# A merge stage whose stationary operand is swapped: activations stay in TensorE, weights stream

## The chip, the cores and the metric

The kernel runs on one core of one Trainium2 chip. The metric is the device time of one launch, in microseconds (us). Three runs of the kernel before gave 2219.97, 2220.11 and 2220.32 us; the median is 2220.11 us.

## The reference, cut to what matters

One layer works on 256 tokens of width 2048: a half-step SwiGLU feed-forward network (FFN), a token mixer, and a second such FFN, each with RMSNorm before and after it. The mixer has three branches (forgetting attention of width 1024, differential attention of 512, memory cross-attention of 512). The part that is changed merges them:

```python
gates = jax.nn.sigmoid(h @ w_merge_gate[l] + b_merge_gate[l])      # [256, 3 * 2048]
g_fox, g_diff, g_mem = jnp.split(gates, 3, axis=-1)
merged = (g_fox * (y_fox @ w_branch_fox[l])
          + g_diff * (y_diff @ w_branch_diff[l])
          + g_mem * (y_mem @ w_branch_mem[l]))                     # [256, 2048]
x = x + rmsnorm(merged @ w_out[l], mix_post_g[l])
```

## The kernel before

Every weight is float32 in memory and is multiplied in three passes: it is split into `hi` (rounded to the float32r format that TensorE multiplies) and `lo = raw - hi`, the activations are held split in the same way, and hi·hi, hi·lo and lo·hi are summed in PSUM. `Stream` does the splitting for all weights in one fixed order. SP (SyncE's queue) loads 1 MB tiles into 3 `raw` buffers (L71); each tile makes two pieces; for a piece ACT (ScalarE) casts `hi` (L94) and DVE (VectorE) subtracts `lo` (L95) into one of 4 split buffers. `ahead()` queues splits of pieces up to 4 beyond the last one released, and `load()` queues the raw tile that follows. So on every engine the order is that of the code: a split stands in the queue behind whatever was written before it, and waits there for the split buffer that PE (TensorE) has to release.

A product takes one of two forms. `mm_a` (L214, L216) keeps 128x128 of the weight stationary and streams the activations: one matmul of 512 columns (both halves of the activation, 256 tokens each) with `hi`, one of 256 columns with `lo`. Its result has channels on partitions, so it can be the next product's operand. `mm_b` (L241 to L243) keeps 128 tokens of an activation stationary and streams 512 columns of the weight: three matmuls for each token half, 12 for a piece. Its result has tokens on partitions and must be turned before it can be the next operand. The FFNs do that in `ffn_up`: DVE transposes 32x32 blocks (L443), `regroup` (L449) moves them with 16 small DMAs on SP, and `split` casts and subtracts (L297, L298). These steps are put into the next product of the FFN, after its pieces 1 and 6.

The mixer's `qk` products, its gates and its branch products use `mm_a`; the order is 16 rounds over blocks of 128 channels (`m`), each with three gate products (16 k-tiles each) and 16 k-tiles of branch products. `lr_sum` (L419, L421) adds the two halves of a bank, `times_row` (L428) multiplies by the token scale, L963 applies the sigmoid with the bias as a column, and L966, L968 multiply and add. `split_to` (L297, L298) writes the merged block `mT`, which the output product `PostProj("out", ...)` then reads k-tile by k-tile. Attention steps (`Fillers`) are slipped in after half products until the first gates are done. `h2T`, `y_a` and `y_b` begin 8 elements behind a 256-byte line (`OFF`), the `v` weights 28 elements behind one (`OFF_V`). Small row vectors such as `g_row` (L375) are loaded by DMAs that ACT issues.

Of the kernel before, what the change touches and what calls it, by code (L numbers as in the profile page):

```python
# [26 lines left out]
LAM_INIT = 0.8 - 0.6 * math.exp(-0.3 * 0)  # L27
NEG = -1e30


LINE = 256
OFF = 8
OFF_V = 28

C_G1, C_GM, C_GMEM, C_G2, C_B, C_HG = 0, 16, 32, 48, 64, 112
N_COLS = 113


class Stream:
# [78 lines left out]
def tile_block(ctx, tc, x, mem, f1gu, f1d, wqk, wv, wmkv, wgate, wbr, wout, f2gu, f2d,  # L118
# [42 lines left out]
        st.add("v", wv[i])  # L161
    for i in range(20):
        st.add("qk", wqk[i])
    for m in range(KT):
        for b in range(3):
            st.add("gate", wgate[b * KT + m])
        st.add("br", wbr[m])
    for i in range(16):
        st.add("out", wout[i], extra={12: (1,), 13: (0, 1)}.get(i, ()))
    add_up(2, f2gu)  # L170
# [30 lines left out]

    fill = Fillers(3, 2)

    def rows_of(pool, n, off, **kw):

        t = pool.tile([P, n * 2 * S + OFF], F32R, align_bytes=LINE, **kw)
        return t[:, off:off + n * 2 * S].rearrange("p (k s n) -> p k s n", k=n, s=2)


    def mm_a(bank, w, kk, act, k, start, stop):  # L210
# [7 lines left out]
    def new_bank(name):  # L218
        return mmp.tile([P, 512], F32, tag="mm", name=name)

    def proj_a(name, act):
        bank = new_bank("mm_a")
        for half in range(2):
            st.ahead()
            w, = st.take(name)
            for kk in range(8):
                k = half * 8 + kk
                mm_a(bank, w, kk, act, k, k == 0, k == KT - 1)
            st.release()
            fill()  # L230
        return bank
# [62 lines left out]
    def split_to(hi, lo, src, scale=None):  # L294

        if scale is None:
            nc.scalar.copy(out=hi, in_=src)  # L297
            nc.vector.tensor_tensor(out=lo, in0=src, in1=hi.bitcast(F32), op=ALU.subtract)  # L298
        else:
            nc.scalar.activation(out=hi, in_=src, func=AF.Copy, scale=scale)  # L300
            nc.vector.scalar_tensor_tensor(out=lo, in0=src, scalar=scale, in1=hi.bitcast(F32),
                                           op0=ALU.mult, op1=ALU.subtract)
# [113 lines left out]
    def lr_sum(dst, bank, tmp_pool, scale=1.0):  # L416

        left = tmp_pool.tile([P, S], F32, tag="left", name="left", bufs=2)
        nc.scalar.activation(out=left, in_=bank[:, 0:S], func=AF.Copy, scale=scale)  # L419
        if scale == 1.0:  # L420
            nc.vector.tensor_tensor(out=dst, in0=bank[:, S:2 * S], in1=left, op=ALU.add)  # L421
        else:
            nc.vector.scalar_tensor_tensor(out=dst, in0=bank[:, S:2 * S], scalar=scale, in1=left,
                                           op0=ALU.mult, op1=ALU.add)

    def times_row(dst, row):
        if row is not None:
            nc.vector.tensor_tensor(out=dst, in0=dst, in1=row, op=ALU.mult)  # L428


    def ffn_up(idx, hT, rstd, setup, groups, inserts):

        state = {}

        def gated(t, bank):
            nc.scalar.activation(out=state["s"][:, t], in_=bank, func=AF.Silu, scale=rstd[t])

        def product(t, bank):

            sg = state["s"]  # L440
            nc.vector.scalar_tensor_tensor(out=sg[:, t], in0=bank, scalar=rstd[t], in1=sg[:, t],
                                           op0=ALU.mult, op1=ALU.mult)
            nc.vector.transpose(out=state["z"][:, t], in_=sg[:, t])  # L443

        def regroup():

            for a in range(4):
                for q in range(4):
                    nc.sync.dma_start(out=state["w"][32 * q:32 * q + 32, :, a],  # L449
                                      in_=state["z"][32 * a:32 * a + 32, :, P * q:P * (q + 1)])  # L450

        def split(n):
            src = state["w"].rearrange("p t a (k i) -> p k (t a) i", k=4)
            hi, lo = (state["gh"][:, 4 * n:4 * n + 4, i].rearrange("p k (g i) -> p k g i", i=32) for i in range(2))
            for k in range(4):
                split_to(hi[:, k], lo[:, k], src[:, k])

        def open_block():
            for name, shape in (("s", [P, 2, 512]), ("z", [P, 2, 512]), ("w", [P, 2, 4, P])):
                state[name] = state["tp"].tile(shape, F32, tag="f" + name, name="f" + name, bufs=1)  # L460

        late = {}
        for n in range(FB):
            if n == 0:
                bg, bu = proj_b2(f"gu{idx}", hT, groups, inserts)
                state["tp"], state["gh"] = setup()
                open_block()
                for t in range(2):
                    gated(t, bg[t])
            else:  # L470
                bg = proj_b(f"gate{idx}", hT, KT, 512, steps=late)
                open_block()
                for t in range(2):
                    gated(t, bg[t])
                bu = proj_b(f"up{idx}", hT, KT, 512)
            for t in range(2):
                product(t, bu[t])
            late = {1: regroup, 6: lambda n=n: split(n)}
        return state["gh"], late


# [2 lines left out]
    hpool = h1_stack.enter_context(tc.tile_pool(name="hT1", bufs=1, side="right", reuse_waits="tile"))  # L484
    gp1 = g1_stack.enter_context(tc.tile_pool(name="gh1", bufs=1, side="left", reuse_waits="tile"))
    tp1 = g1_stack.enter_context(tc.tile_pool(name="ft1", bufs=1, side="left", reuse_waits="tile"))
    hT1 = rows_of(hpool, KT, 0, name="hT1")
    gh1 = rows_of(gp1, FT, 0, name="gh1")
    zeros = hpool.tile([P, 512], BF16, name="zeros")
    nc.vector.memset(zeros, 0.0)  # L490

# [48 lines left out]
    yap = ya_stack.enter_context(tc.tile_pool(name="yap", bufs=1, side="right", reuse_waits="tile"))  # L540
    fg_stack = ExitStack()
    fgp = fg_stack.enter_context(tc.tile_pool(name="fg1", bufs=1, side="right", reuse_waits="tile"))
    mha = rows_of(yap, 8, 0, tag="y", name="mha")
    macc = [small.tile([P, 4], F32, name=f"macc{t}", bufs=1) for t in range(2)]
    order = [(c, t) for c in range(4) for t in range(2)]
    mem_c = {}
# [27 lines left out]
    h2_stack = ExitStack()  # L574
    h2p = h2_stack.enter_context(tc.tile_pool(name="h2p", bufs=1, side="left", reuse_waits="tile"))
    ybp = yb_stack.enter_context(tc.tile_pool(name="ybp", bufs=1, side="left", reuse_waits="tile"))
    h2T = rows_of(h2p, KT, OFF, tag="h", name="h2T")
    mhb = rows_of(ybp, 8, 0, tag="y", name="mhb")

    def x1_update(i):  # L580
        if i < 8:
# [166 lines left out]

        return [s1, s2]

    y_a = rows_of(yap, 8, OFF, tag="y", name="y_a")
    y_b = rows_of(ybp, 8, OFF, tag="y", name="y_b")

    def softmax_stats(s_aps, tag="e", bufs=6):

# [175 lines left out]
            fill.add(mem_unit(h // 2, head("mq", sc)), 2)  # L931


    mg_stack = ExitStack()
    mT = None
    for m in range(KT):
        zs = []
        for b in range(3):
            z = zp.tile([P, S], F32, tag="z", name="z", bufs=4)
            lr_sum(z, proj_a("gate", h2T), zp)  # L940
            times_row(z, hrow)
            zs.append(z)
        if m == 0:
            while fill.left():
                fill(drain=True)
            at_stack.close()
            mgp = mg_stack.enter_context(tc.tile_pool(name="mgp", bufs=1, side="left", reuse_waits="tile"))
            mT = rows_of(mgp, KT, 0, name="mT")
        bb = [new_bank("mm_br") for _ in range(3)]
        lims = [(0, 8), (8, 12), (12, 16)]  # L950
        for half in range(2):
            st.ahead()
            w, = st.take("br")
            for kk in range(8):
                k = half * 8 + kk
                i = 0 if k < 8 else (1 if k < 12 else 2)
                mm_a(bb[i], w, kk, (y_a, y_b)[half], kk, k == lims[i][0], k == lims[i][1] - 1)
            st.release()
        acc = None
        for b in range(3):  # L960
            g = zs[b]
            c = C_B + b * KT + m
            nc.scalar.activation(out=g, in_=g, func=AF.Sigmoid, bias=colt[:, c:c + 1])  # L963
            br = zp.tile([P, S], F32, tag="br", name="br")
            lr_sum(br, bb[b], zp)
            nc.vector.tensor_tensor(out=g, in0=br, in1=g, op=ALU.mult)  # L966
            if acc is not None:
                nc.vector.tensor_tensor(out=g, in0=acc, in1=g, op=ALU.add)  # L968
            acc = g
        split_to(mT[:, m, 0], mT[:, m, 1], acc)  # L970
    mix.close()
    ya_stack.close()


    h3T = rows_of(h2p, KT, 0, tag="h", name="h3T")
    fg_stack = ExitStack()
    fgp = fg_stack.enter_context(tc.tile_pool(name="fgm", bufs=1, side="right", reuse_waits="tile"))
    st.extra_pool = fg_stack.enter_context(tc.tile_pool(name="xsplit", bufs=st.extra_bufs, side="right", reuse_waits="tile"))
# [9 lines left out]
        for c in range(4):  # L988
            post2.update(0, c)

    post2.body()
    banks = post2.last(lag=7, first_done=first_half,
                       inserts={1: lambda: x2_in(0, 0)(), 2: lambda: x2_in(0, 1)(), 3: lambda: st.ahead(2),
                                5: lambda: st.ahead(2)})
# [4 lines left out]
    def setup2():  # L999
        fg_stack.close()  # L1000
        mg_stack.close()
        yb_stack.close()
        gp = g2_stack.enter_context(tc.tile_pool(name="gh2", bufs=1, side="right", reuse_waits="tile"))
        tp = g2_stack.enter_context(tc.tile_pool(name="ft2", bufs=1, side="right", reuse_waits="tile"))
        return tp, rows_of(gp, FT, 0, name="gh2")

    gh2, late2 = ffn_up(2, h3T, h3r, setup2, [[0, 1]] + [[i] for i in range(2, 8)],
                        {(1, 0): lambda: (x2_in(1, 0, 2)(), post2.update(1, 1)),
# [109 lines left out]
```

## Time and profile before

| | |
|---|---|
| median of 3 runs | 2220.11 us |
| profiled execution, its own time | 2220.04 us |
| its span | 2218.2 us (1.8 us lie around it) |
| PE matmul busy | 2208.0 us, 100% of the span |
| DVE, ACT busy | 1288.2 us (58%), 1037.0 us (47%) |
| TensorE clock granted | 0.999 of full speed (2.4 GHz) |
| DMA engines, mean busy share | about half of the span in every slice |

A busy PE means that matmuls were under way, and their records overlap; what a matmul costs is the distance from its start to the next one's start, and is read from places far apart and a count between them.

### The profile page before, as it was taken

The numbers are of one execution on the slowest core, as the hardware profiler recorded it, in microseconds if no ns is written. First come the engines' busy times: TensorE is split into PE (matmuls) and PEld (weight loads), VectorE is DVE, ScalarE is ACT, GpSimd is POOL, SyncE is SP. The second block draws the span as 40 slices with busy tenths as digits, with TensorE's granted clock in tenths as the row PEclk, the third lists the DMA queues.
The fourth block names the chain that finished last, engine by engine and source line by source line (L and its number), as shares of the span: only waits on it lengthen the run. The fifth ranks groups of instructions, "written<-read, shape, count | busy, mean of one in ns | idle before, by whom it ended". The sixth has DMA issues, their size and how long they took to land. (4 is left out here: it accounts for less than half of the span.)

```text
span 2218.2 us, 27157 instructions
## 1 busy us (share of the span) xinstructions
PE 2208.0 (100%) x10625; PEld 1869.7 (84%) x10625; DVE 1288.2 (58%) x1625; ACT 1037.0 (47%) x1484; POOL 13.5 (1%) x25
## 2 busy tenths in 40 slices
PE   9999999999999999999999999999999999999998
PEld 7888888888888899988888888888888888888887
DVE  5555555555444756766776767566555555554444
ACT  6444444445344644544555555446444444444442
POOL 0000000000000000000000000000000000000000
PEclk9999999999999999999999999999999999999999
DMA  7565556566555454544555555654655565565553
GB/s 265 189 220 202 200 190 234 199 217 219 193 201 202 160 194 152 183 161 143 190 177 203 177 203 177 212 199 161 236 200 203 197 219 207 187 225 199 201 202 133
DMA packets 91793, 434.51 MB, mean 196 GB/s; under 512 B 13072, under 2 KB 35984, under 8 KB 44304
## 3 DMA queue, kind: packets, MB, share of 16 engines
q1 hardware_dynamic: 87200, 425.84, 54.9%
q10 hardware_dynamic: 4464, 6.93, 1.0%
q8 instruction: 83, 1.36, 0.2%
q14 instruction: 46, 0.38, 0.1%
HBM read 419.09 MB, written 2.10 MB: 190 GB/s over the span
## 5 line engine op out<-in xcount | busy, mean ns | idle before, releaser
L95 DVE TENSOR_TENSOR lo<-raw,hi 128x1024 fp32r<-128x1024 f32 (+2 forms) x794 | 957.0, 1211 | 760.2 <-ACT hi L94 756.3
L94 ACT CAST hi<-raw 128x1024 fp32r<-128x1024 f32 (+2 forms) x794 | 819.2, 1037 | 871.6 <-PE mm_b L243 761.9
L214 PE MATMUL mm_a<-h2T,hi 128*128 128x512 f32 x1088 | 384.0, 394 | 0.0
L216 PE MATMUL mm_a<-h2T,lo 128*128 128x256 f32 x1088 | 306.5, 282 | 0.0
L241 PE MATMUL mm_b<-hi,hT 128*128 128x512 f32 x704 | 274.3, 390 | 0.2 <-ACT hi L94 0.2
L241 PE MATMUL mm_b<-hi,h3T 128*128 128x512 f32 x704 | 274.5, 390 | 0.0
L242 PE MATMUL mm_b<-lo,hT 128*128 128x512 f32 x704 | 274.0, 389 | 0.5 <-DVE lo L95 0.5
L241 PE MATMUL mm_b<-hi,gh 128*128 128x512 f32 x704 | 274.2, 390 | 0.0
L243 PE MATMUL mm_b<-hi,h3T 128*128 128x512 f32 x704 | 274.0, 389 | 0.0
L243 PE MATMUL mm_b<-hi,hT 128*128 128x512 f32 x704 | 273.9, 389 | 0.0
L242 PE MATMUL mm_b<-lo,h3T 128*128 128x512 f32 x704 | 273.9, 389 | 0.0
L243 PE MATMUL mm_b<-hi,gh 128*128 128x512 f32 x704 | 273.9, 389 | 0.0
L242 PE MATMUL mm_b<-lo,gh 128*128 128x512 f32 x704 | 273.8, 389 | 0.0
L214 PEld LDWEIGHTS mm_a<-h2T,hi 128*128 128x128 f32 x1088 | 204.3, 188 | 42.1
L216 PEld LDWEIGHTS mm_a<-h2T,lo 128*128 128x128 f32 x1088 | 205.7, 189 | 0.2
L241 PEld LDWEIGHTS mm_b<-hi,hT 128*128 128x128 f32 x704 | 132.1, 188 | 28.2 <-ACT hi L94 0.7
L242 PEld LDWEIGHTS mm_b<-lo,hT 128*128 128x128 f32 x704 | 132.1, 188 | 28.1 <-DVE lo L95 0.8
L243 PEld LDWEIGHTS mm_b<-hi,gh 128*128 128x128 f32 x704 | 132.2, 188 | 27.6
L242 PEld LDWEIGHTS mm_b<-lo,h3T 128*128 128x128 f32 x704 | 132.2, 188 | 27.4
L243 PEld LDWEIGHTS mm_b<-hi,h3T 128*128 128x128 f32 x704 | 132.2, 188 | 27.4
L243 PEld LDWEIGHTS mm_b<-hi,hT 128*128 128x128 f32 x704 | 132.1, 188 | 27.4
L242 PEld LDWEIGHTS mm_b<-lo,gh 128*128 128x128 f32 x704 | 132.2, 188 | 27.3
(210 smaller groups left out, 1963.4 us busy)
## 6 DMA issues: line engine op xcount, KB each, us to landing
raw<-in_f2gu SPq DMA_DIRECT2D x88, 1024.0 KB, 5.0
raw<-in_f1gu SPq DMA_DIRECT2D x86, 1024.0 KB, 5.0
raw<-in_wgate SPq DMA_DIRECT2D x48, 1024.0 KB, 4.9
raw<-in_f1d SPq DMA_DIRECT2D x44, 1024.0 KB, 4.8
raw<-in_f2d SPq DMA_DIRECT2D x44, 1024.0 KB, 4.8
raw<-in_wv SPq DMA_DIRECT2D x24, 856.0 KB, 4.5
raw<-in_wqk SPq DMA_DIRECT2D x20, 1024.0 KB, 4.8
raw<-in_wbr SPq DMA_DIRECT2D x16, 1024.0 KB, 4.8
```

Of the source, the lines that this page charges most:

```text
L94: self.nc.scalar.copy(out=hi[:, i], in_=src[:, i])
L95: self.nc.vector.tensor_tensor(out=lo[:, i], in0=src[:, i], in1=hi[:, i].bitcast(F32), op=ALU.subtract)
L214: nc.tensor.matmul(bank, lhsT=hi[:, i, c], rhs=act[:, k].rearrange("p s n -> p (s n)"), start=start, stop=False)
L216: nc.tensor.matmul(bank[:, 0:S], lhsT=lo[:, i, c], rhs=act[:, k, 0], start=False, stop=stop)
L241: nc.tensor.matmul(o, lhsT=xh, rhs=wh, start=start and kk == 0, stop=False)
L242: nc.tensor.matmul(o, lhsT=xh, rhs=wl, start=False, stop=False)
L243: nc.tensor.matmul(o, lhsT=xl, rhs=wh, start=False, stop=stop and kk == 1)
```

## The change

Gates and branch products take the form `mm_b`. The loop now runs over 4 blocks of 512 channels (`n`), and in each over the three branches: a gate product (8 pieces), its bias row by a DMA that ACT issues, scale and bias on DVE, the sigmoid on ACT, then the branch product (4, 2 and 2 pieces), its multiplication with the gate and the sum on DVE. At a block's end DVE transposes the sum into `z` (named `mz` in rows), and `turned_block`, which is the FFN's `regroup` and `split` taken out as a function, moves and splits it inside the next product: the 16 DMAs after piece 0, the split after piece 4. For the last block the next product is the output product. The offsets `OFF` go, `OFF_V` becomes 20, the weights are laid out anew on the host, and the bias is given as rows in the turned order.

```diff
-OFF = 8
-OFF_V = 28
+OFF_V = 20
...
+    def turned_block(z, w, dst, n, at=(1, 6)):
+        def regroup():
+            for a in range(4):
+                for q in range(4):
+                    nc.sync.dma_start(out=w[32 * q:32 * q + 32, :, a],
+                                      in_=z[32 * a:32 * a + 32, :, P * q:P * (q + 1)])
+        def split():
+            src = w.rearrange("p t a (k i) -> p k (t a) i", k=4)
+            hi, lo = (dst[:, 4 * n:4 * n + 4, i].rearrange("p k (g i) -> p k g i", i=32) for i in range(2))
+            for k in range(4):
+                split_to(hi[:, k], lo[:, k], src[:, k])
+        return {at[0]: regroup, at[1]: split}
...
-    for m in range(KT):
-        zs = []
-        for b in range(3):
-            z = zp.tile([P, S], F32, tag="z", name="z", bufs=4)
-            lr_sum(z, proj_a("gate", h2T), zp)
-            times_row(z, hrow)
-            zs.append(z)
...
-                mm_a(bb[i], w, kk, (y_a, y_b)[half], kk, k == lims[i][0], k == lims[i][1] - 1)
...
+    late = {}
+    for n in range(4):
+        acc = None
+        for b, y in enumerate((y_a, y_b[:, 0:4], y_b[:, 4:8])):
+            banks = proj_b("gate", h2T, KT, 512, steps=late)
+            late = {}
...
+            bias = mwp.tile([P, 512], F32, tag="bias", name="bias", bufs=2)
+            nc.scalar.dma_start(out=bias, in_=rows[3 + b:4 + b, 512 * n:512 * (n + 1)].partition_broadcast(P)[:, 0])
+            g = mwp.tile([P, 2, 512], F32, tag="g", name="g", bufs=2)
+            for t in range(2):
+                nc.vector.scalar_tensor_tensor(out=g[:, t], in0=banks[t], scalar=hr[t], in1=bias,
+                                               op0=ALU.mult, op1=ALU.add)
+                nc.scalar.activation(out=g[:, t], in_=g[:, t], func=AF.Sigmoid)
+            banks = proj_b("br", y, 8 if b == 0 else 4, 512)
...
+            for t in range(2):
+                o = acc[:, t] if b == 0 else g[:, t]
+                nc.vector.tensor_tensor(out=o, in0=banks[t], in1=g[:, t], op=ALU.mult)
+                if b:
+                    nc.vector.tensor_tensor(out=acc[:, t], in0=acc[:, t], in1=g[:, t], op=ALU.add)
+        for t in range(2):
+            nc.vector.transpose(out=z[:, t], in_=acc[:, t])
+        late = turned_block(z, w, mT, n, (0, 4))
...
-    post2.body()
+    post2.body(late)
```

Three places show how the queues change. The first is ACT around the first merged channels of the kernel before, from the last casts ahead of the sigmoid (`z` is a gate) to the split of the merged block:

```order
L94 CAST hi<-raw 128x1024 x2
L963 ACT_TABLE_LOAD
L963 ACTIVATE z<-z,colt 128x256
L419 ACTIVATE left<-mm_br 128x256
L963 ACTIVATE z<-z,colt 128x256
L419 ACTIVATE left<-mm_br 128x256
L963 ACTIVATE z<-z,colt 128x256
L419 ACTIVATE left<-mm_br 128x256
L297 CAST mT<-z 128x256
```

The second is ACT of the changed kernel from the third gate of a block (its bias, its sigmoid) to the first gate of the next block:

```order
L956 DMA bias<-in_rows 128x512
L961 ACTIVATE g<-g 128x512 x2
L92 CAST hi<-raw 128x1024 x7
L297 CAST mT<-mw 128x256 x4
L92 CAST hi<-raw 128x1024 x3
L956 DMA bias<-in_rows 128x512
L961 ACTIVATE g<-g 128x512 x2
```

Four casts of the merged block now stand together between casts of weight pieces 7 and 8 of the next gate, and they read `mw`, which DMAs fill; before, one cast of 128 channels stood right behind DVE's sum.

The third is DVE of the changed kernel over the same stretch, from the third gate of a block to the first gate of the next:

```order
L959 SCALAR_TENSOR_TENSOR g<-mm_b,rstd_tok,bias 128x512 x2
L93 TENSOR_TENSOR lo<-raw,hi 128x1024 x2
L967 TENSOR_TENSOR g<-mm_b,g 128x512
L969 TENSOR_TENSOR acc<-acc,g 128x512
L967 TENSOR_TENSOR g<-mm_b,g 128x512
L969 TENSOR_TENSOR acc<-acc,g 128x512
L971 STREAM_TRANSPOSE mz<-acc 128x512 x2
L93 TENSOR_TENSOR lo<-raw,hi 128x1024 x5
L298 TENSOR_TENSOR mT<-mw,mT 128x256 x4
L93 TENSOR_TENSOR lo<-raw,hi 128x1024 x3
L959 SCALAR_TENSOR_TENSOR g<-mm_b,rstd_tok,bias 128x512 x2
```

The gate's scale and bias now need the bias row that ACT's DMA brings, and the sum and the transposes stand behind two splits.

## Rows read from the trace of the kernel before

**Rows 1.** The page, parts 1 and 4: busy time, and the chain that ended last.

```profile
PE 2208.0 (100%) x10625; PEld 1869.7 (84%) x10625; DVE 1288.2 (58%) x1625; ACT 1037.0 (47%) x1484; POOL 13.5 (1%) x25
...
PE 32%; issue 0%; DVE 0%; ACT 0%; DVEq 0%; POOLq 0%; POOL 0%
```

**Rows 2.** Busy time by stretch; this one is the merge stage.

```profile
1040.57:1400.68 360.11, 360.11 (x2084) 319.28 (x2083) 253.24 (x379) 188.30 (x299) 0.00 (x0) 1.00 0.54 186
```

**Rows 3.** ACT in order of time, second FFN, two products' border at 1579.66.

```profile
1576.94 1.05 ACT L94 CAST hi<-raw 128x1024 fp32r<-128x1024 f32 x1 [1.67 <-PE mm_b L243]
1579.66 1.05 ACT L94 CAST hi<-raw 128x1024 fp32r<-128x1024 f32 x1 [1.67 <-PE mm_b L243]
...
1595.98 1.05 ACT L94 CAST hi<-raw 128x1024 fp32r<-128x1024 f32 x1 [1.67 <-PE mm_b L243]
1596.93 1.32 ACT L297 CAST gh<-fw 128x256 fp32r<-128x256 f32 x4
```

**Rows 4.** DVE in order of time, the same border.

```profile
1578.02 1.23 DVE L95 TENSOR_TENSOR lo<-raw,hi 128x1024 fp32r<-128x1024 f32 x1 [1.49 <-ACT hi L94]
1579.16 0.74 DVE L441 SCALAR_TENSOR_TENSOR fs<-mm_b,rstd_tok,fs 128x512 f32<-128x512 f32 x1
...
1580.58 0.71 DVE L441 SCALAR_TENSOR_TENSOR fs<-mm_b,rstd_tok,fs 128x512 f32<-128x512 f32 x1
1581.32 0.71 DVE L443 STREAM_TRANSPOSE fz<-fs 128x512 f32<-128x512 f32 x1
1581.96 1.18 DVE L95 TENSOR_TENSOR lo<-raw,hi 128x1024 fp32r<-128x1024 f32 x1
```

**Rows 5.** SP's queue in order of time, the same border.

```profile
1571.12 12.38 SPq L71 DMA_DIRECT2D raw<-in_f2gu  x3
1583.55 10.83 SPq L449 DMA_DIRECT2D fw<-fz  x16
1594.48 15.04 SPq L71 DMA_DIRECT2D raw<-in_f2gu  x5
```

**Rows 6.** Tile `mm_br`: durations (ns), first and last start (us) of its `hi` matmuls.

```profile
L214 PE MATMUL mm_br<-y_a,hi x128: 390/390/583, 1062.1 to 1397.6; 128*128 128x512 f32 x128
```

**Rows 7.** ACT in order of time in the `v` products (428 columns).

```profile
807.36 0.91 ACT L94 CAST hi<-raw 128x856 fp32r<-128x856 f32 x1 [1.40 <-PE mm_b L243]
...
816.59 0.91 ACT L94 CAST hi<-raw 128x856 fp32r<-128x856 f32 x1 [1.41 <-PE mm_b L243]
```

**Rows 8.** DMA issues: count, KB each, median us from issue to landing.

```profile
raw<-in_wgate SPq DMA_DIRECT2D x48, 1024.0 KB, 4.9
...
fw<-fz SPq DMA_DIRECT2D x352, 32.0 KB, 1.9
...
g_row<-in_rows ACTq DMA_DIRECT2D x12, 256.0 KB, 3.2
```

**Rows 9.** Tile `g_row`: landing of its 12 row loads.

```profile
DMA to landing us min/median/max: 3.2/3.2/6.2
```

**Rows 10.** SP's queue at 739 to 744 us.

```profile
741.71 0.33 SPq L71 DMA_DIRECT2D raw<-in_wmkv  x1
```

**Rows 11.** Tile `mem_c` at 742.4 to 742.9 us: one load of 256 KB.

```profile
L552 ACTq DMA_DIRECT2D mem_c<-in_mem x1: 334/334/334, 742.5 to 742.5; - x1
...
DMA to landing us min/median/max: 5.2/5.2/5.2
```

**Rows 12.** Groups by line: count, busy us, mean ns, idle before.

```profile
L436 ACT ACTIVATE fs<-mm_b,rstd_tok 128x512 f32<-128x512 f32 x44 | 29.2, 683 | 4.5 <-PE mm_b L243 3.5 <-POOL rstd_tok L305 0.9
...
L963 ACT ACTIVATE z<-z,colt 128x256 f32<-128x256 f32 x48 | 24.0, 501 | 0.0
...
L379 DVE TENSOR_TENSOR fg<-mm_b,g_row 128x512 f32<-128x512 f32 x24 | 15.6, 682 | 0.0
...
L346 DVE TENSOR_TENSOR h2T<-tg,h2T 128x512 fp32r<-128x512 f32 x8 | 5.5, 692 | 0.3
```

**Rows 13.** Tile `fw`: duration (ns) of one of its DMA issues on SP.

```profile
L449 SPq DMA_DIRECT2D fw<-fz x352: 585/595/1495, 59.4 to 1985.2; - x176
```

More of the change, by code (lines that the diff above doesn't have):

```diff
@@ L31 @@
 LINE = 256
-OFF = 8
-OFF_V = 28
-C_G1, C_GM, C_GMEM, C_G2, C_B, C_HG = 0, 16, 32, 48, 64, 112
-N_COLS = 113
+OFF_V = 20
+C_G1, C_GM, C_GMEM, C_G2, C_HG = 0, 16, 32, 48, 64
+N_COLS = 65
 class Stream:
@@ L163, in tile_block @@
         st.add("qk", wqk[i])
-    for m in range(KT):
-        for b in range(3):
-            st.add("gate", wgate[b * KT + m])
-        st.add("br", wbr[m])
+    for n in range(4):
+        for b, (lo, hi) in enumerate(((0, 2), (2, 3), (3, 4))):
+            for i in range(4):
+                st.add("gate", wgate[(4 * b + n) * 4 + i])
+            for i in range(lo, hi):
+                st.add("br", wbr[4 * n + i])
     for i in range(16):
@@ L202, in tile_block, with rows_of @@
     fill = Fillers(3, 2)
-    def rows_of(pool, n, off, **kw):
-        t = pool.tile([P, n * 2 * S + OFF], F32R, align_bytes=LINE, **kw)
-        return t[:, off:off + n * 2 * S].rearrange("p (k s n) -> p k s n", k=n, s=2)
+    def rows_of(pool, n, **kw):
+        t = pool.tile([P, n * 2 * S], F32R, align_bytes=LINE, **kw)
+        return t.rearrange("p (k s n) -> p k s n", k=n, s=2)
     def mm_a(bank, w, kk, act, k, start, stop):
@@ L443, in product @@
             nc.vector.transpose(out=state["z"][:, t], in_=sg[:, t])
[L445 to L456, printed above, removed]
         def open_block():
@@ L477, in ffn_up @@
                 product(t, bu[t])
-            late = {1: regroup, 6: lambda n=n: split(n)}
+            late = turned_block(state["z"], state["w"], state["gh"], n)
         return state["gh"], late
@@ L486, in tile_block @@
     tp1 = g1_stack.enter_context(tc.tile_pool(name="ft1", bufs=1, side="left", reuse_waits="tile"))
-    hT1 = rows_of(hpool, KT, 0, name="hT1")
-    gh1 = rows_of(gp1, FT, 0, name="gh1")
+    hT1 = rows_of(hpool, KT, name="hT1")
+    gh1 = rows_of(gp1, FT, name="gh1")
     zeros = hpool.tile([P, 512], BF16, name="zeros")
@@ L542, in tile_block @@
     fgp = fg_stack.enter_context(tc.tile_pool(name="fg1", bufs=1, side="right", reuse_waits="tile"))
-    mha = rows_of(yap, 8, 0, tag="y", name="mha")
+    mha = rows_of(yap, 8, tag="y", name="mha")
     macc = [small.tile([P, 4], F32, name=f"macc{t}", bufs=1) for t in range(2)]
@@ L576, in tile_block @@
     ybp = yb_stack.enter_context(tc.tile_pool(name="ybp", bufs=1, side="left", reuse_waits="tile"))
-    h2T = rows_of(h2p, KT, OFF, tag="h", name="h2T")
-    mhb = rows_of(ybp, 8, 0, tag="y", name="mhb")
+    h2T = rows_of(h2p, KT, tag="h", name="h2T")
+    mhb = rows_of(ybp, 8, tag="y", name="mhb")
     def x1_update(i):
@@ L749, in forget_gate @@
         return [s1, s2]
-    y_a = rows_of(yap, 8, OFF, tag="y", name="y_a")
-    y_b = rows_of(ybp, 8, OFF, tag="y", name="y_b")
+    y_a = rows_of(yap, 8, tag="y", name="y_a")
+    y_b = rows_of(ybp, 8, tag="y", name="y_b")
     def softmax_stats(s_aps, tag="e", bufs=6):
@@ L931, in tile_block @@
             fill.add(mem_unit(h // 2, head("mq", sc)), 2)
-    mg_stack = ExitStack()
-    mT = None
-    for m in range(KT):
-        zs = []
-        for b in range(3):
-            z = zp.tile([P, S], F32, tag="z", name="z", bufs=4)
-            lr_sum(z, proj_a("gate", h2T), zp)
-            times_row(z, hrow)
-            zs.append(z)
[L943 to L956, printed above, removed]
-                mm_a(bb[i], w, kk, (y_a, y_b)[half], kk, k == lims[i][0], k == lims[i][1] - 1)
-            st.release()
-        acc = None
[L960 to L970, printed above, removed]
@@ new lines, in tile_block @@
+    mg_stack, mw_stack = ExitStack(), ExitStack()
+    late = {}
+    for n in range(4):
+        acc = None
+        for b, y in enumerate((y_a, y_b[:, 0:4], y_b[:, 4:8])):
+            banks = proj_b("gate", h2T, KT, 512, steps=late)
+            late = {}
+            if n == b == 0:
+                while fill.left():
+                    fill(drain=True)
+                at_stack.close()
+                mgp = mg_stack.enter_context(tc.tile_pool(name="mgp", bufs=1, side="left", reuse_waits="tile"))
+                mT = rows_of(mgp, KT, name="mT")
+                z = mgp.tile([P, 2, 512], F32, name="mz")
+                w = mgp.tile([P, 2, 4, P], F32, name="mw")
+                mwp = mw_stack.enter_context(tc.tile_pool(name="mwp", bufs=1, side="left", reuse_waits="tile"))
+            bias = mwp.tile([P, 512], F32, tag="bias", name="bias", bufs=2)
[6 more added lines that the diff above has]
+            banks = proj_b("br", y, 8 if b == 0 else 4, 512)
+            if acc is None:
+                acc = mwp.tile([P, 2, 512], F32, tag="acc", name="acc")
+            for t in range(2):
[6 more added lines that the diff above has]
+        late = turned_block(z, w, mT, n, (0, 4))
@@ L971, in tile_block @@
+    mw_stack.close()
     mix.close()
     ya_stack.close()
-    h3T = rows_of(h2p, KT, 0, tag="h", name="h3T")
+    h3T = rows_of(h2p, KT, tag="h", name="h3T")
     fg_stack = ExitStack()
@@ L1004, in setup2 @@
         tp = g2_stack.enter_context(tc.tile_pool(name="ft2", bufs=1, side="right", reuse_waits="tile"))
-        return tp, rows_of(gp, FT, 0, name="gh2")
+        return tp, rows_of(gp, FT, name="gh2")
     gh2, late2 = ffn_up(2, h3T, h3r, setup2, [[0, 1]] + [[i] for i in range(2, 8)],
@@ L1068 @@
     cols = np.concatenate([col(W["ffn1_pre_g"]), col(W["mix_pre_g"]), col(W["mem_norm_g"]), col(W["ffn2_pre_g"]),
-                           col(W["b_merge_gate"]), col(W["diff_head_g"])], axis=1)
-    rows = np.stack([W["ffn1_post_g"], W["mix_post_g"], W["ffn2_post_g"]])
+                           col(W["diff_head_g"])], axis=1)
+    turned = lambda v: v.reshape(-1, 4, 4, 32).transpose(0, 2, 1, 3).reshape(-1, D)
+    rows = np.concatenate([np.stack([W["ffn1_post_g"], W["mix_post_g"], W["ffn2_post_g"]]),
+                           turned(W["b_merge_gate"])])
     lamv = np.stack([W["diff_lambda_q1"], W["diff_lambda_k1"], W["diff_lambda_q2"], W["diff_lambda_k2"]])
@@ L1097 @@
         "wmkv": _tiles_b(np.concatenate([W["w_mem_kv"][:, 512:], W["w_mem_kv"][:, :512]], axis=1), 512),
-        "wgate": _tiles_a(W["w_merge_gate"]),
-        "wbr": _tiles_a(np.concatenate([W["w_branch_fox"], W["w_branch_diff"], W["w_branch_mem"]], axis=0)),
+        "wgate": _tiles_up(W["w_merge_gate"]),
+        "wbr": _tiles_up(np.concatenate([W["w_branch_fox"], W["w_branch_diff"], W["w_branch_mem"]], axis=0)),
         "wout": _tiles_b(W["w_out"], 512),
```

## The prediction

> **What bounds the kernel now.** First the page's busy line and chain: PE has matmuls under way in 2208.0 of 2218.2 us, DVE and ACT are at 58% and 47%, and the chain names hardly anything but PE [rows 1]. The listing by stretch says the same of the stage that is changed: 360.11 us, PE busy in all of it, the clock at full speed, 2.4 GHz [rows 2]. The kernel does not wait there; only fewer or cheaper matmuls can make it shorter, and a wait that the change brings is lost time. So I look for two numbers: what a product costs on PE in either form, and whether DVE, ACT and SP still deliver in time. The second is read at a border between two FFN products, where `regroup` and `split` run today: ACT casts a piece every 2.72 us, each time when PE lets go of a buffer [rows 3], DVE does the products and transposes in between [rows 4], SP issues 16 small DMAs in one go [rows 5].
>
> **The matmuls.** For 128 channels and one k-tile `mm_a` streams 512 + 256 columns in 2 matmuls, `mm_b` for 512 channels 6 x 512 in 6: the same 768 columns for 128 channels, but 1.5 matmuls in place of 2. `mm_a`: between the first and the last start of `y_a`'s `hi` matmuls, 335.5 us, lie 15 rounds of 64 pairs and 7 pairs, 967 in all: 0.347 us a pair [rows 6]. The stage has 1,024 pairs: 355.3 us. (The stretch of 360.1 also holds attention steps, which stay.) `mm_b`: a piece of 12 matmuls takes 19.04 / 7 = 2.72 us [rows 3], and 128 pieces take 348.2 us. **Gain 7.1 us.** Per matmul, 0.347 us is 768 columns at 2.4 GHz and twice 13.5 ns, and 2.72 us is 6,144 columns and 12 times 13.3 ns: the gain is 512 matmuls fewer at some 13.5 ns each. The Trainium skill (TensorE: Matmul & The Clock Gate, section on the missing 2.5 ns) gives a warm matmul N / 2.4 GHz and about 2.5 ns; by that the 512 would be worth 1.3 us. These float32r rows differ from it, and I go by the rows.
>
> Removed on DVE and ACT: `lr_sum`, `times_row` and the casts for 16 channel blocks. PE hid them; worth nothing. The offsets: `qk` keeps 640 `mm_a` matmuls and `v` 576 `mm_b` ones, now with `h2T` at the line's start. A `v` piece takes 9.23 / 4 = 2.31 us [rows 7], 14 ns a matmul above its 428 columns, 1 ns from the others. I take 0, and 1,216 x 1 ns = 1.2 us to either side.
>
> **A gate's end.** Let G be the end of a gate product. The last split queued ahead of it has its cast at G - 2.7 and its `lo` until G - 0.4 (as 1576.94 and 1578.02 stand to 1579.66 [rows 3, 4]). Behind that cast ACT issues the bias DMA, about G - 1.8. The nearest row is `g_row`, the same 256 KB out of the same tensor: 3.2 us [rows 8], so G + 1.4 at best; but one of 12 took 6.2 [rows 9]. What else is in flight? A raw tile is issued when the `lo` before has ended, G - 3.1, and lands 4.9 later [rows 8], G + 1.8. `mem_c`, issued 0.76 us after a raw tile [rows 10, 11], took 5.2 us, about 1 us beyond that tile's landing. A bias issued 1.3 us after one is nearer to this case than to the median: I take G + 2.8, bounds G + 1.4 and G + 4.4 (6.2 from issue).
>
> The Trainium skill (DMA: Bandwidth & Descriptors, section on queues, rings and completion order) says that each DMA engine takes turns between its queues packet by packet. By that the small load would not wait for the big one, and the bias would land at about 3.2 us; this is the first rival below.
>
> DVE then needs 0.73 twice (L441 is the same operation) [rows 4], to G + 4.3; the second sigmoid of 512 columns (between 0.50 for 256 and 0.68 for another function of 512 [rows 12]; I take 0.75) ends at G + 5.0. Behind it the next cast ends at G + 6.0, its `lo` at G + 7.2, needed when PE begins the fourth piece on, G + 8.2. No stall: 1 us to spare.
>
> **A block's end.** The third branch has 2 pieces, so PE ends the block at T = G + 5.4. DVE has one more `lo` (G + 8.4), four products and sums of 512 columns at 0.68 (0.682 and 0.692 [rows 12]) to G + 11.1, two transposes to G + 12.4: **`z` is done at T + 7.0**. In the FFN it is at 1582.03, T + 2.4 [rows 4]. From there the FFN's rows apply, as the DMAs are of the same form: a `lo`, a raw issue, then regroup starts 1.5 after `z`, takes 10.8 [rows 4, 5], and the last of the 16, issued 0.6 before the end [rows 13], lands 1.9 later [rows 8]. That is `z` + 13.6: **T + 20.6** here, T + 16.0 in the FFN, where the casts stand at 1596.93, T + 17.3, behind the cast of piece 9 [rows 3], and nothing waits. Here they stand two pieces earlier, behind the cast of piece 7, which ends at T + 12. So **ACT's queue waits from T + 12 to T + 20.6**, with the casts of pieces 8, 9 and 10 and the next bias behind it; SP has also held back raw tiles by 10.8 us. Then 4 casts (1.3), the cast of piece 8 (1.0), its `lo` (1.2): T + 24.1. PE has used up its lead at piece 8, T + 21.8, and waits at that piece's second matmul, T + 22.0: **2.1 us lost**, three times: 6.3 us. The late bias behind it (issued near T + 24, landed 3.2 later, then the chain above) costs at most 0.3 more at the piece after next: 0.2 each time, 0.6.
>
> The fourth time the next product is the output product, whose piece 6 (T + 16.3) reads this block. Its first cast ends at T + 21.0: **4.7 us**, and it delays everything behind it, so piece 8 is then in time.
>
> Sum: 6.3 + 0.6 + 4.7 - 7.1 = **+4.5 us**. Against the profiled execution's own 2220.04 (span 2218.2 and 1.8 around it; the median is 2220.11) that is **2224.5 us**, 0.2% slower, just where a measurement of this kernel begins to tell it from no change (0.2%, 4.4 us).
>
> **Rivals.** *The bias is not late* (3.2 us). Everything behind it moves forward by 1.4: `z` at T + 5.6, landing T + 19.2. Stalls 0.7 three times and 3.3: 5.4 - 7.1, 2218.3. For: 3.2 is the median. Against: the raw tile in flight, and the 5.2 of [rows 11].
>
> *Nothing waits.* It decides at `z` = T + 4.9 for the gate products (T + 4.9 + 13.6 + 3.5 = T + 22.0) and at T + 2.3 for the output product. For: the FFN pays nothing for the same DMAs. Against: DVE has six operations where the FFN has four, behind a wait. If DVE keeps up and the 16 issues go faster, PE keeps its 7.1: 2213.0, faster.
>
> *The bias is later still*, G + 4.4, as the 6.2 of [rows 9]: each stall grows by 1.6, and `lo` of piece 3 in the new block (behind `z`, done at G + 15.2, needed at G + 13.6) adds 1.6 at each of four borders: 4.5 + 4 x 1.6 + 4 x 1.6 = +17, 2237. Full size is not likely, as raw tiles come only every 5.4 us.
>
> *The form is not cheaper*: if these products did not reach the rate of the FFN's pieces, the 7.1 would fall away and the stalls stay, 2231.6. The FFN's pieces, of the same shape and the same four buffers, speak against it; it shares the chance of the case before.
>
> **How the numbers follow.** Forecast case (bias near G + 2.8, four stalls of 7 to 15 us together) 0.48: 0.20 of it within 0.2%, 0.28 slower. Bias in time 0.22, within 0.2%. Nothing waits 0.15, faster. Later still or no gain 0.15, slower. So faster 0.15, same 0.42, slower 0.43. The range reaches from the case without waits, 2213, to 2232, about half way into the last case; within the forecast case alone it is 2220 to 2228.
>
> **What would show it.** Right: matmuls of the merge stage 13.3 ns above their columns each; casts of `mT` that wait for DMA `mw` (some 8 us each time) on ACT; PE waiting for `lo` at the first piece of the `br` products of blocks 2 to 4, some 2 us, and for `mT` at piece 6 of the output product, 4 to 5 us; DVE waiting for the bias at each gate, landed 4 to 5 us after issue. Wrong: `mw` landed when ACT comes to it, so that the page's chain is PE alone; or PE waiting at every gate, not only at block borders; or `qk` and `v` at another rate per matmul than now.

## The result, and the profile after

The changed kernel takes 2234.36 us (median of 6 runs, 2232.47 to 2235.75) against 2220.12 us before: 1.0063 times as long, interval 1.0052 to 1.0075. It is 14.2 us slower. The profiled execution took 2234.84 us, its span is 2233.0 us, 14.8 us more than before, and these 14.8 us are what has to be found.

First the page of the changed kernel, parts 1 and 4, to be read beside [rows 1]. PE has 512 instructions fewer, as the change says, but its share fell to 99%: 23 us of the span are now without a matmul, where 10 were. The chain still names PE alone, so it doesn't show the waits; the stretches do.

```profile
PE 2209.7 (99%) x10113; PEld 1847.4 (83%) x10113; DVE 1243.2 (56%) x1473; ACT 1001.8 (45%) x1364; POOL 13.5 (1%) x25
...
PE 32%; DVE 0%; ACT 0%; DVEq 0%; POOLq 0%; issue 0%; ACTq 0%
```

Busy time by stretch of the kernel before, the `qk` products and the output product (the merge stage between them is [rows 2]). The columns are the stretch, its length, busy time of PE, PEld, DVE, ACT and POOL, the granted clock, the DMA share and GB/s:

```profile
905.13:1040.57 135.44, 135.44 (x820) 120.00 (x818) 91.49 (x169) 61.42 (x127) 1.38 (x2) 1.00 0.47 163
1400.68:1488.69 88.01, 88.01 (x395) 72.83 (x393) 50.98 (x60) 41.23 (x58) 0.56 (x1) 1.00 0.56 198
```

The same view of the changed kernel: `qk`, the merge stage, the output product, 4 us at the border of blocks 1 and 2, and 9 us within the output product:

```profile
905.86:1042.81 136.95, 136.95 (x819) 120.10 (x818) 91.63 (x169) 61.57 (x127) 1.38 (x2) 1.00 0.45 160
1042.81:1409.00 366.19, 358.07 (x1573) 293.86 (x1572) 204.10 (x222) 151.87 (x176) 0.00 (x0) 1.00 0.55 194
1409.00:1503.30 94.30, 89.87 (x393) 73.87 (x392) 54.98 (x64) 42.70 (x61) 0.56 (x1) 0.98 0.56 195
...
1160.00:1164.00 4.00, 4.00 (x12) 3.12 (x11) 1.91 (x2) 0.65 (x1) 0.00 (x0) 0.57 0.96 254
1425.00:1430.00 5.00, 0.57 (x4) 0.15 (x2) 0.12 (x1) 0.55 (x2) 0.00 (x0) 1.00 0.35 67
1430.00:1434.00 4.00, 4.00 (x11) 3.10 (x12) 3.56 (x6) 2.67 (x5) 0.00 (x0) 0.57 0.98 414
```

`qk` takes 1.5 us more, the merge stage 6.1, the output product 6.3: 13.9 of the 14.8. `qk` also begins 0.7 us later, and what follows the output product is 0.2 us longer. In the merge stage PE is without work for 8.1 us, where it had none such.

What waits, in the two stages (engine and line, what it waited for, us in total, times, longest):

```profile
ACT mT L297 <- DMA mw<-mz: 34.1, 4, 8.7
DVE g L959 <- DMA bias<-in_rows: 31.7, 11, 3.4
...
PE mm_b L241 <- ACT mT L297: 4.4, 1, 4.4
PE mm_b L241 <- ACT hi L92: 4.3, 5, 1.2
PE mm_b L242 <- DVE lo L93: 3.8, 5, 0.8
```

PE waits five times for `hi` and `lo` of a weight piece: once in the first branch product of blocks 2, 3 and 4, as forecast, and once more in blocks 3 and 4. The chain behind that is read at the end of the first block. PE in order of time, with the second wait of block 3 and the wait in the output product below:

```profile
1135.29 0.39 PE L241 MATMUL mm_b<-hi,h2T 128*128 128x512 f32 x1
...
1156.82 0.39 PE L243 MATMUL mm_b<-hi,h2T 128*128 128x512 f32 x1
1158.42 0.50 PE L241 MATMUL mm_b<-hi,y_a 128*128 128x512 f32 x1 [1.21 <-ACT hi L92]
1159.68 0.51 PE L242 MATMUL mm_b<-lo,y_a 128*128 128x512 f32 x1 [0.76 <-DVE lo L93]
...
1160.50 0.59 PE L242 MATMUL mm_b<-lo,y_a 128*128 128x512 f32 x1
...
1259.53 0.50 PE L241 MATMUL mm_b<-hi,y_a 128*128 128x512 f32 x1 [0.60 <-ACT hi L92]
1260.79 0.50 PE L242 MATMUL mm_b<-lo,y_a 128*128 128x512 f32 x1 [0.76 <-DVE lo L93]
...
1425.09 0.39 PE L243 MATMUL mm_b<-hi,mT 128*128 128x512 f32 x1
1429.90 0.58 PE L241 MATMUL mm_b<-hi,mT 128*128 128x512 f32 x1 [4.43 <-ACT mT L297]
1430.29 0.63 PE L242 MATMUL mm_b<-lo,mT 128*128 128x512 f32 x1
```

DVE in order of time:

```profile
1132.59 1.41 DVE L959 SCALAR_TENSOR_TENSOR g<-mm_b,rstd_tok,bias 128x512 f32<-128x512 f32 x2 [2.96 <-DMA bias<-in_rows]
...
1140.57 1.30 DVE L971 STREAM_TRANSPOSE mz<-acc 128x512 f32<-128x512 f32 x2
...
1164.22 1.41 DVE L959 SCALAR_TENSOR_TENSOR g<-mm_b,rstd_tok,bias 128x512 f32<-128x512 f32 x2 [2.32 <-DMA bias<-in_rows]
```

SP's queue in order of time:

```profile
1143.38 11.08 SPq L437 DMA_DIRECT2D mw<-mz  x16
1154.56 0.53 SPq L69 DMA_DIRECT2D raw<-in_wbr  x1
1155.19 15.93 SPq L69 DMA_DIRECT2D raw<-in_wgate  x4
```

ACT in order of time:

```profile
1127.34 0.34 ACTq L956 DMA_DIRECT2D bias<-in_rows  x1
...
1156.10 1.33 ACT L297 CAST mT<-mw 128x256 fp32r<-128x256 f32 x4 [8.68 <-DMA mw<-mz]
1157.33 1.99 ACT L92 CAST hi<-raw 128x1024 fp32r<-128x1024 f32 x2
1159.60 1.05 ACT L92 CAST hi<-raw 128x1024 fp32r<-128x1024 f32 x1 [0.28 <-DMA raw<-in_wbr]
1159.62 0.33 ACTq L956 DMA_DIRECT2D bias<-in_rows  x1
1165.01 1.29 ACT L961 ACTIVATE g<-g 128x512 f32<-128x512 f32 x2 [4.36 <-DVE g L959]
```

The block ends at T = 1135.29, with the first matmul on `h2T`. DVE got the bias at 1132.59 and ends the transposes at 1141.87, T + 6.6. SP's 16 issues follow until 1154.46, the last of them lands by 1156.1, T + 20.8, and ACT has stood for 8.68 us by then. PE runs dry at 1157.05, where the gate product ends. The cast at 1159.60 waits for a raw tile that SP could issue only behind the 16 small DMAs (1154.56), and the next bias is issued behind that cast, at 1159.62, 2.6 us after the gate's end. It lands about 1164.2.

What a wait costs: a matmul after a wait stands at 0.50 us, where the next one usually starts 0.23 us on, so the cost is the idle time and 0.27 us. The first wait is then 1.21 + 0.76 + 0.54 = 2.5 us in block 2 (2.3 and 2.4 in the others), the second 1.9 us in block 3 (1.7 in block 4). In block 2 the place of the second wait is taken by a fall of the clock: from 1160.50 to about 1164 matmuls start 0.42 us apart, the 1.2 GHz level (granted clock 0.57 from 1160 to 1164), and some 1.6 us are lost. That makes 12.4 us at the three borders. In the output product the wait is 1429.90 - 1425.09 - 0.23 = 4.6 us; PE was busy for 0.57 of the 5.00 us ahead of 1430, and then the granted clock over 4 us is 0.57. Nine matmuls from 1429.90 to 1433.66 cost 0.42 us each in place of 0.23: 1.7 us more.

### The profile page after: what moved, and what is told of

Its sections match the earlier page's. It is cut to its first block, busy times and chain, and to the rows that moved or that the text cites. A ratio compares the mean times of both kernels' runs of the same rounds, so it can differ in the third digit from the quotient of the medians.

```text
span 2233.0 us, 25894 instructions
## 1 busy us (share of the span) xinstructions
PE 2209.7 (99%) x10113; PEld 1847.4 (83%) x10113; DVE 1243.2 (56%) x1473; ACT 1001.8 (45%) x1364; POOL 13.5 (1%) x25
## 5 line engine op out<-in xcount | busy, mean ns | idle before, releaser
L241 PE MATMUL mm_b<-hi,h2T 128*128 128x512 f32 (+1 forms) x576 | 220.5, 383 | 0.0
L242 PE MATMUL mm_b<-lo,h2T 128*128 128x512 f32 (+1 forms) x576 | 218.1, 379 | 0.3 <-DVE lo L93 0.3
L243 PE MATMUL mm_b<-hi,h2T 128*128 128x512 f32 (+1 forms) x576 | 217.9, 378 | 0.0
L243 PEld LDWEIGHTS mm_b<-hi,gh 128*128 128x128 f32 x704 | 132.3, 188 | 27.4
L243 PEld LDWEIGHTS mm_b<-hi,h3T 128*128 128x128 f32 x704 | 132.3, 188 | 27.4
L241 PEld LDWEIGHTS mm_b<-hi,h3T 128*128 128x128 f32 x704 | 132.3, 188 | 27.2
L241 PEld LDWEIGHTS mm_b<-hi,gh 128*128 128x128 f32 x704 | 132.3, 188 | 27.1
```

The costliest lines, as they stand in the source:

```text
L241: nc.tensor.matmul(o, lhsT=xh, rhs=wh, start=start and kk == 0, stop=False)
L242: nc.tensor.matmul(o, lhsT=xh, rhs=wl, start=False, stop=False)
L243: nc.tensor.matmul(o, lhsT=xl, rhs=wh, start=False, stop=stop and kk == 1)
```

## The experiments

Two theories stood after the result. One: ACT's queue is what hurts, the four casts that wait for `mw` with the weight casts and the bias behind them. The rival: the late `z` and SP's 11 us of issues, which delay `mw` and the next raw tile alike, so that the place of the casts is not the point.

**The split moved later.** The casts of the merged block stand behind piece 1 of the branch product, the DMAs where they were; the output product keeps the changed kernel's places.

```diff
-            banks = proj_b("gate", h2T, KT, 512, steps=late)
-            late = {}
+            banks = proj_b("gate", h2T, KT, 512, steps={0: late[0]} if late else {})
...
-            banks = proj_b("br", y, 8 if b == 0 else 4, 512)
+            banks = proj_b("br", y, 8 if b == 0 else 4, 512, steps={1: late[4]} if late else {})
+            late = {}
```

> Only the split of blocks 1 to 3 is moved, from behind piece 4 of the next gate product to behind piece 1 of the branch product after it; the 16 small DMAs, the bias loads and the last block stay as in the changed kernel. Theory (the four casts that wait on ACT for the small DMAs hold up the casts of weight pieces behind them): the three stretches of lost time of 4.1 to 4.3 us at the first branch product of blocks 2 to 4 go, some 12.6 us, and the output product still waits 4.6 us at piece 6: 2234.4 - 12.6 = about 2222 us. Rival (the weight tiles that SP holds back behind its 16 issues are what comes late): SP's queue is unchanged, so at least two thirds of the loss stay, 2230 us or more.

Measured: 2240.32 us, 1.0091 (1.0076 to 1.0106), slower than the changed kernel. ACT of this kernel in order of time:

```profile
1159.12 1.05 ACT L92 CAST hi<-raw 128x1024 fp32r<-128x1024 f32 x1 [6.59 <-DMA raw<-in_wbr]
1159.14 0.34 ACTq L955 DMA_DIRECT2D bias<-in_rows  x1
```

Its merge stage by stretch, and what PE waits for there:

```profile
1042.48:1413.67 371.19, 360.77 (x1572) 296.47 (x1571) 204.17 (x222) 152.06 (x176) 0.00 (x0) 0.98 0.54 192
```

```profile
PE mm_b L241 <- ACT hi L92: 8.4, 3, 3.0
```

The wait for `mw` is gone from the weight casts, and in its place the cast of piece 10 waits 6.59 us for a raw tile that SP issued late. The bias stands behind that cast and is as late as before (1159.14 against 1159.62). PE now comes to its fourth branch piece in time to wait up to 3.0 us for it in one go, and the clock falls at every border (matmuls start 0.43 us apart behind each of these waits). The first theory alone has fallen: what ACT waits for behind SP's 16 issues can be exchanged, not avoided.

**The bias issued ahead of its gate product.** Only the place of the load moves; one bias buffer of two is free there.

```diff
+            if n or b:
+                bias = load_bias(n, b)
             banks = proj_b("gate", h2T, KT, 512, steps=late)
...
-            bias = mwp.tile([P, 512], F32, tag="bias", name="bias", bufs=2)
-            nc.scalar.dma_start(out=bias, in_=rows[3 + b:4 + b, 512 * n:512 * (n + 1)].partition_broadcast(P)[:, 0])
+            if n == b == 0:
+                bias = load_bias(n, b)
```

> Only the bias load is moved, ahead of the gate product that it belongs to (the very first stays). Theory (the bias that lands 2.5 to 3 us after a gate's end puts off everything behind it on DVE): the transposes end at T + 4 in place of T + 6.6, the small DMAs land at T + 17.9, the first piece of the branch product is in time; the 12.6 us at the three borders go, the output product's wait shrinks from 4.6 to 2 us: 2234.4 - 12.6 - 2.6 = 2219 us, or 2217.5 if the clock does not fall there any more. Rival (the lateness comes from DVE's own operations and the small DMAs, and the bias is covered by them): 2231 us or more.

Measured: 2219.52 us, 0.9995 (0.9985 to 1.0004): 14.8 us less than the changed kernel by one moved load. Merge stage and output product by stretch:

```profile
1042.61:1396.20 353.59, 353.59 (x1572) 292.89 (x1570) 208.09 (x225) 154.78 (x177) 0.00 (x0) 1.00 0.59 202
1396.20:1488.20 92.00, 89.92 (x393) 73.80 (x392) 52.63 (x62) 41.61 (x59) 0.56 (x1) 0.98 0.56 198
```

PE never waits in the merge stage. It takes 353.6 us, 6.5 less than in [rows 2]: that is the gain of the matmul form by itself, and 366.2 - 353.6 = 12.6 us is what the three borders cost, against the 12.4 us added up above. `z` is done 2.9 us earlier, at T + 3.7. In the output product 4.0 of 6.3 us stay: a wait of 2.1 us and a fallen clock.

**Both moves together.**

```diff
+            if n or b:
+                bias = load_bias(n, b)
+            banks = proj_b("gate", h2T, KT, 512, steps={0: late[0]} if late else {})
...
+            banks = proj_b("br", y, 8 if b == 0 else 4, 512, steps={1: late[4]} if late else {})
```

> Both moves: the bias load ahead of its gate product and the split of blocks 1 to 3 in the branch product. Theory after the first runs (the bias load, issued by ACT behind a cast that waits for a raw tile, is what turns a late cast into 4 us of lost time; the casts of mT that wait until T + 18 cost nothing by themselves): 2219.5 us, as with the early bias alone, and 21 us less than with the late split alone. Rival (the waiting casts still cost something with the early bias): 2217 us or less.

Measured: 2217.89 us, 0.9991 (0.9981 to 1.0). The merge stage is 353.6 us again; the output product takes 90.3 us with a wait of 2.0 us, and no fallen clock in the profiled execution. With the bias early, PE waits as before wherever the split stands: nowhere in the merge stage, and 2 us in the output product. The median is 1.6 us below that of the early bias alone, between the two expectations, but that need not come from the split: most executions of either kernel lie near 2217.7 or near 2219.6 us, and of the two that were profiled the one at 2219.7 (early bias alone) has the fallen clock, the one at 2217.81 has not.

**Two queues for the last block.** To the early bias, the last block's 16 DMAs are issued half by SP and half by GpSimd.

```diff
-                    nc.sync.dma_start(out=w[32 * q:32 * q + 32, :, a],
+                    queues[q % len(queues)].dma_start(out=w[32 * q:32 * q + 32, :, a],
...
+        late = turned_block(z, w, mT, n, (0, 4), (nc.sync, nc.gpsimd) if n == 3 else (nc.sync,))
```

> The early bias, and for the last block the 16 small DMAs shared between SP and GpSimd's queue, 8 each. Theory (the output product waits because one queue takes 11 us to issue 16 small DMAs): SP is done near T + 10.5, the merged block is split before piece 6 at T + 16.3, the wait of 2.1 us and the slow clock behind it go, 4 us: 2215.5 us, faster than the kernel before. Rival (GpSimd's issues take as long as what they save, or land late; no row shows them): 2219.5 us or more.

Measured: 2215.84 us, 0.9979 (0.9971 to 0.9988). The output product by stretch:

```profile
1396.60:1484.60 88.00, 88.00 (x393) 72.81 (x392) 52.71 (x62) 41.71 (x59) 4.96 (x9) 1.00 0.59 206
```

It has the 88.0 us of the kernel before; SP spends 6.12 us on its eight issues. So the wait in the output product and its fallen clock, 6.3 us in the changed kernel, come from when the block arrives, and from nothing else.

**Two queues in all blocks, bias late, and bias early.** The first is the changed kernel with `(nc.sync, nc.gpsimd)` for every block and nothing else; the second adds the early bias.

```diff
-        late = turned_block(z, w, mT, n, (0, 4))
+        late = turned_block(z, w, mT, n, (0, 4), (nc.sync, nc.gpsimd))
```

> The changed kernel with its late bias, and in all four blocks the 16 small DMAs shared between SP and GpSimd's queue; nothing else. Theory (the loss needs both the late transposes and the 11 us in which SP issues): SP is done some 5 us earlier, so the small DMAs land near T + 16.5 (they ended at T + 13.7 with the early bias, whose transposes end 2.9 earlier), the next raw tile 5 us earlier too, and no piece at the borders is late; the output product waits about 1 us at its piece 6. 2234.4 - 12.6 - 5.3 = 2216.5 us. Rival (the late bias costs PE by itself, whatever SP does): 2228 us or more.

> The early bias and the two queues in all four blocks. Theory: PE waits nowhere in the merge stage any more, as with two queues in the last block alone, 2215.8 us. Rival (raw tiles that come earlier, or DMAs issued by GpSimd, bring something else): different by more than 1.5 us.

Measured: 2217.11 us, 0.9986 (0.9977 to 0.9996), with the late bias; 2215.71 us, 0.998 (0.997 to 0.9989), with the early one. Tile `mw` of the first: durations of the issues on either queue (ns), and who waited for the tile:

```profile
L437 POOL DMA_DIRECT2D mw<-mz x32: 533/536/700, 1143.1 to 1408.0; - x32
L437 SPq DMA_DIRECT2D mw<-mz x32: 585/596/748, 1143.9 to 1410.4; - x32
...
  ACT mT L297: 18.7, 4
...
  PE mm_b L241: 1.0, 1
```

With the bias as late as in the changed kernel (`z` at T + 6.4) the merge stage takes 353.6 us, and only the output product still waits, 1.0 us (89.4 us). Either remedy removes all 12.6 us at the borders, so neither cause does it alone: it takes a `z` 3 us late and 11 us of issues behind it. (The next gate's bias also goes out earlier here, at T + 19.7 in place of T + 24.3, as ACT is held for 4.4 us and not for 8.7.) The version with both and the one ahead of it (2215.84) are equal within their spread and the fastest that were run; 2215.71 is 4.4 us under the kernel before.

**Keeping the clock.** The changed kernel, with 18 matmuls on zeros, whose result nobody reads, in front of the piece of the output product that waits.

```diff
+    late[5] = lambda: keep_clock2(18)
```

> The changed kernel with 18 matmuls on zeros, their result unused, between pieces 5 and 6 of the first output product, where PE waits 4.6 us; they fill some 3.9 us of the wait. Theory (the 427 ns matmuls behind the wait are TensorE at half clock because it idled, some 1.7 us): the output stage takes 92.7 us, not 94.3, 2232.8 us. Rival (they are slow for another reason, operands or transfers): no change, 2234.4 us.

Measured: 2232.30 us, 1.0054 (1.004 to 1.0068). Stretches around the wait:

```profile
1423.00:1428.00 5.00, 5.00 (x25) 2.74 (x24) 0.00 (x0) 0.00 (x0) 0.00 (x0) 1.00 0.20 52
...
1432.00:1436.00 4.00, 4.00 (x19) 3.30 (x19) 3.71 (x5) 1.49 (x2) 0.00 (x0) 1.00 0.93 326
```

The granted clock stays at 1.00 and no matmul behind the wait is slow, so the 1.7 us worked out above are gone. The output product takes 93.1 us, only 1.2 less than the 94.3 of the changed kernel, because the wait costs 5.0 us in this run and cost 4.6 there.

**The offsets, back in the changed kernel, and away from the kernel before.** The diff of the first is shown; the second sets `OFF` to 0 and `OFF_V` to 20 in the kernel before.

```diff
-OFF_V = 20
+OFF = 8
+OFF_V = 28
...
-    h2T = rows_of(h2p, KT, tag="h", name="h2T")
+    h2T = rows_of(h2p, KT, OFF, tag="h", name="h2T")
```

> Only the offsets are put back: h2T begins 8 elements behind a 256-byte line and the v weights 28, as in the kernel before; the merge stage stays as changed. Theory (the offsets cost the qk products 1.5 us): 2234.4 - 1.5 = about 2233 us, and in the trace the qk matmuls with hi are at 228 ns again, not 233 to 241. Rival (the 1.5 us are attention steps that fall differently): 2234.4 us and the same distances as in the changed kernel.

> The kernel before with its offsets taken away (h2T, y_a, y_b at a line's start, v weights 20 behind one), nothing else. Theory (a line's start costs each pair of mm_a some 4.7 ns): 320 pairs of qk and 1,024 of the merge stage give 6.3 us, 2226.4 us. Rival (no cost): 2220.1 us.

Measured: the changed kernel with offsets 2236.94 us, 1.0074 (1.0059 to 1.0089); the kernel before without them 2222.00 us, 1.0008 (0.9999 to 1.0018). First the changed kernel with offsets, `qk` and the merge stage by stretch:

```profile
905.26:1040.70 135.44, 135.44 (x819) 120.00 (x818) 91.52 (x169) 61.48 (x127) 1.38 (x2) 1.00 0.45 162
1040.71:1411.46 370.75, 364.25 (x1572) 292.51 (x1571) 204.23 (x222) 152.12 (x177) 0.00 (x0) 1.00 0.55 192
```

The kernel before without offsets, the same stretches:

```profile
906.08:1043.03 136.95, 136.95 (x819) 119.91 (x818) 91.67 (x169) 61.62 (x127) 1.38 (x2) 1.00 0.47 160
1043.03:1403.38 360.35, 360.35 (x2085) 317.65 (x2084) 253.28 (x379) 188.26 (x299) 0.00 (x0) 1.00 0.54 186
```

PE of the first in a gate product, two matmuls with four others between them:

```profile
1100.07 0.40 PE L242 MATMUL mm_b<-hi,h2T 128*128 128x512 f32 x1
...
1101.23 0.40 PE L244 MATMUL mm_b<-hi,h2T 128*128 128x512 f32 x1
```

`qk` is 135.44 us with offsets and 136.95 without, in both kernels: the removal costs `qk` 1.5 us, and this is the term that I took as nothing. But the gate products need it. With `h2T` 8 elements behind a line five matmuls take 1.16 us, 0.232 each (0.2333 over a whole gate product), where the changed kernel has 0.2266; the 1,152 gate matmuls would cost 7.7 us more, more than the 6.5 the form gains. So neither expectation held: with the offsets back `qk` gives back its 1.5 us, and the gates take more than that. The branch products of the same run, whose `y_b` stays at a line's start, have 0.2265 with it. In `mm_a`, where `h2T` streams, the same offset in the merge stage is worth 0.2 us only: the kernel before without offsets is 1.8 us slower, not the 6.3 of its theory and not the 0 of the rival. Why `qk` alone pays among the `mm_a` products was not settled. Nor does the place of the stationary operand decide alone: the `v` products hold the same `h2T` stationary and take 124.9 us with it 8 elements behind a line and with it at the line's start, but there their weights moved along, from 28 elements behind a line to 20. Whether the distance between the two operands is what counts, no run shows.

## Why the prediction was wrong, step by step

**The gain of 7.1 us: right.** The merge stage without waits is 353.6 us, 6.5 less than before. That is 12.7 ns for each of the 512 matmuls, near the 13.3 to 13.5 of the rows. By the Trainium skill (TensorE: Matmul & The Clock Gate, section "Wait — 56ns, not 53.3ns?"), which gives about 2.5 ns a matmul, they would have been worth an estimated 1.3 us; the measured 6.5 decides.

**The first wait: right, in part by luck.** The bias landed at G + 2.7 (G is 1129.85 in the third gate; predicted G + 2.8), `z` at T + 6.6 (7.0), `mw` at T + 20.8 (20.6), and 2.3 to 2.5 us lost at piece 8 (2.1). But it was issued at 1127.34, G - 2.5, where I had G - 1.8, and took 5.2 us, where I had 4.6; and `z` was 0.4 us early while its way to the last landing took 14.2 us in place of 13.6. Both pairs of errors nearly cancel. The rival of a bias in time, 3.2 us from issue, did not hold. Tile `bias` of the changed kernel, landing of its 12 loads:

```profile
DMA to landing us min/median/max: 3.3/5.1/5.6
```

The Trainium skill (DMA: Bandwidth & Descriptors, section "Queues, rings and completion order") says that each DMA engine takes turns between its queues packet by packet. From that the rival took a landing in about 3.2 us; the measured 5.1 decides against the 3.2, but whether the engines took turns can't be told from a landing.

**What stands behind the first wait: this step failed.** The prediction put the late bias there at "at most 0.3 more", 0.2 each time, with a landing 3.2 us after its issue. The issue came where I had it (T + 24.3), but the cast ahead of it had waited for a raw tile just landed, the next raw tiles were in flight, and the bias took 4.6 us to 5.4 us. I had used the slower landing for the quiet gate and the median for the crowded one. With it the first cast of the fourth branch piece ends at 1259.50 in block 3, and PE starts at 1259.53: 1.9 and 1.7 us more in two blocks. ACT of block 3 in order of time, and DVE:

```profile
1251.04 0.33 ACTq L956 DMA_DIRECT2D bias<-in_rows  x1
...
1258.45 3.88 ACT L92 CAST hi<-raw 128x1024 fp32r<-128x1024 f32 x4
```

```profile
1256.47 1.41 DVE L959 SCALAR_TENSOR_TENSOR g<-mm_b,rstd_tok,bias 128x512 f32<-128x512 f32 x2 [3.14 <-DMA bias<-in_rows]
```

A landing after 3.2 us in place of 5.4 would have put this chain 2.2 us earlier, ahead of PE, which comes to the piece at 1258.8. That is an estimate from these rows; no run changed the landing alone.

**The clock was no term of the sum.** It fell in block 2 and in the output product, 1.6 and 1.7 us. The second wait and the clock together are 5.2 us at the borders where I had 0.6. Nothing in the trace of before shows PE waiting for that long, and I did not ask what follows a wait.

**The output product: wait right, size not.** 4.6 us (4.7), and the clock on top.

**The offsets: the term 0, with 1.2 to either side, was mis-sized.** It is +1.5 us in `qk`; `v` takes 124.9 us in both kernels.

In sum the prediction had -7.1 + 6.9 + 4.7 = 4.5; the trace has -6.5 + 12.6 + 6.3 + 1.5 = 13.9, and 0.9 outside these stages, most of it ahead of `qk`. The gain, the first waits (7.2 us for 6.3) and the wait in the output product are each off by 0.9 at most, the offsets by 1.5; what comes after a wait is 6.9 us (5.2 at the borders, 1.7 in the output product) where I had 0.6. The rival "the bias is later still" gave 2237 by a bias at G + 4.4 and stalls grown everywhere; the time came near it, but its mechanism is not what the rows show. "Nothing waits" was reached by mending: -6.5 + 1.5 and what varies at the start give the 4.4 us of the version with both remedies.

## What to carry to other kernels

When a step is moved behind a wait, follow the queue through a second round: what the waiting engine issues next is late as well, and lands in a crowd. A load that needs nothing but a free buffer can be issued one product earlier; here that was worth 14.8 us, and PE paid nothing for it. Count a long run of small DMAs as time during which its queue issues nothing else, and before removing an alignment offset ask which operand it places, in which matmul form, and where the other operand begins.

## What the hardware showed that I had not expected

After a wait of 4.6 us the granted clock had a mean of 0.57 over 4 us, and matmuls came 0.42 us apart; with matmuls on zeros in the wait it stayed at 1.00. After waits that cost 2.3 to 2.5 us it fell in one block and not in two others, and after the last block's wait of 2.1 us it fell in one run, after one of 2.0 us in another it did not. A stationary operand that begins 8 elements behind a 256-byte line costs 6.7 ns a matmul of 512 columns in the gates (0.2333 against 0.2266 us), and nothing in `v`, where the weights are shifted too. A 256 KB load that took 3.2 us in the median for `g_row` [rows 9] took 5.1 here, amid 1 MB loads on another queue. GpSimd issues the small DMA in 0.54 us, SP in 0.60.
